# A decoder layer whose x also comes laid out with features on partitions, and whose vectors come as one table of columns

## The chip, the cores and the metric

One core of one Trainium2 chip runs the kernel. The metric is the device time of one execution in microseconds (us). The host lays weights out before the launch; that is not timed.

Engines: PE is TensorE (PEld its weight loads), DVE is VectorE, ACT is ScalarE, POOL is GpSimd, SP is SyncE, which here only issues DMAs. A queue of DMA issues is marked with a q (SPq, ACTq).

## What is computed

One layer on 256 tokens of 1024 features, in float32:

```
xn = rmsnorm(x, g1)
aq, ak, av, mq, mk, mv, mo, mi, mf, ga, gm = split(xn @ w_in)
ya = attention(aq, ak, av)                        # 8 heads of 64, causal
qk = silu(causal_conv(concat(mq, mk), conv_w, conv_b))
ym = rmsnorm(sigmoid(mo) * mlstm(qk, mv, mi + b_i, mf + b_f), gml)
h  = x + (sigmoid(ga + b) * (ya @ w_up_a) + sigmoid(gm + b) * (ym @ w_up_m)) @ w_out
h  = h + moe(rmsnorm(h, g2))                      # 32 experts, top group, top 2 in it
h  = h + (p @ w_proj) * sigmoid(rmsnorm(h, g3) @ w_gate)
out = rmsnorm(h, g_final)
```

## The kernel before, in words

All loads but one go out on SP's queue in program order. Big tiles live in a ring of ten slots of 2 MB (`slot`), so a late load waits until an earlier tile is done with. DMAs take semaphores in rotation: a new DMA on SP also waits until the one eight places before it has landed.

The front of the kernel is the mixing part. x is loaded in two halves into `h`, with tokens on partitions, between the pieces of the first weight, mq (L73 to L76). PE transposes it, 16 times 128x128, into PSUM (`transpose_x`, L252). For each of the eight k tiles (128 features each, L289) ScalarE scales the transposed x by the norm's gain g1 and rounds it to a high part (L298), VectorE makes the low part, what is left (L299); ScalarE and VectorE split the weights of the tile the same way into `whi` (L304) and `wlo` (L305); and PE multiplies high by high, high by low and low by high (L307 to L309), twelve products of 256 columns for one k tile, into four accumulators `pmq`. `on_act` and `on_dve` fix the order of these on ScalarE and VectorE.

The norm's 1/rms is not needed for that. Squares of `h` are summed on ScalarE (`square_x`, L277, four operations of 128x512), VectorE adds and scales the sums (L280, L189), POOL takes the power (L190), PE spreads the result over a tile (`prt`, L284), VectorE copies it to `rT` (L285), and whatever leaves PSUM later is multiplied by `rT` (L547, L542).

Then come the two gates of the mLSTM (`if_gates`, L384): POOL clears a part of the scratch tile that the squares were written to (L386) and lays the small gate weights out in it (L387, L388), they are split like any others, PE projects them (`pif`, L330 to L332), and a chain of small operations on four partitions on VectorE (L395 to L409), with an exponential and a logarithm on ScalarE (L400, L401), gives `am`, which PE transposes (`pam`, L415). The projections of mk, aq, ak and so on follow (`chunk_T`, `proj_T`), each with splits of 128x512 (L219, L220). A depthwise convolution of the columns of mq and mk runs between them (`conv`, L361 to L367: one ScalarE step and three VectorE steps, `acc`, for each of eight tiles). Where the program leaves the order open, the scheduler sets it.

Vectors (gains, biases, convolution weights) are loaded as 76 rows of 128 (L91), transposed by PE in one go and copied to the table `cols` (`load_columns`, L243); g1 has its own small load and transpose (L68, L234), the gate biases two loads (L101, L102). Before all this PE runs three products of 512 columns on an identity (L230), whose result nobody uses.

After the mixing part comes the expert part: 32 experts, 6 MB of weights each, loaded through the ring, then a last gate and norm.

Of the kernel before, what the change touches and what calls it, by code (L numbers as in the profile page):

```python
# [8 lines left out]
F32 = mybir.dt.float32  # L9
# [5 lines left out]
OP = mybir.AluOpType  # L15
# [19 lines left out]
NWARM0 = 3  # L35
# [12 lines left out]
def layer(ctx: ExitStack, tc: tile.TileContext, A, dbg=None):  # L48
    nc = tc.nc
    mm = nc.tensor.matmul  # L50

    const = ctx.enter_context(tc.tile_pool(name="const", bufs=1))
# [4 lines left out]
    fc = front.enter_context(tc.tile_pool(name="fc", bufs=1))  # L57

    def slot(shape, dt=F32, name="wt"):

        return ring.tile(shape, dt, name=name, tag="ring")


    h = keep.tile([P, NB, D], F32, name="h")
    y = keep.tile([P, NB, D], F32, name="scratch", tag="y")
    x_v = A["x"].rearrange("o (b p) d -> p (o b) d", p=P)
    g1r = fc.tile([KD, P], F32, name="g1r")
    nc.scalar.dma_start(out=g1r, in_=A["mix_norm_g"].rearrange("o (k p) -> (o k) p", p=P))  # L68
# [10 lines left out]
    rows = fc.tile([76, P], F32, name="rows")
    col_of = {}  # L80
    r0 = 0
    for nm, src in (
            ("g2", A["ffn_norm_g"].rearrange("o (k p) -> (o k) p", p=P)),
            ("g3", A["ple_norm_g"].rearrange("o (k p) -> (o k) p", p=P)),
            ("cb", A["conv_b"].rearrange("o (k p) -> (o k) p", p=P)),
            ("cw", A["conv_w"].rearrange("o c (k p) -> (o c k) p", p=P)),
            ("gml", A["mlstm_norm_g"].rearrange("o (k p) -> (o k) p", p=P)),
            ("bg", A["b_gate"].rearrange("o (k p) -> (o k) p", p=P)),
    ):
        n = src.shape[0]  # L90
        nc.sync.dma_start(out=rows[r0:r0 + n], in_=src)  # L91
        col_of[nm] = r0
        r0 += n
# [138 lines left out]

    pg1 = psf.tile([P, 512], F32, name="pg1", tag="tp")
    after(nc.tensor.transpose(pg1[:, 0:KD], g1r, ident[0:KD, 0:KD]), warm0)  # L234
    g1c = fc.tile([P, KD], F32, name="g1c")
    g1_copy = nc.vector.tensor_copy(out=g1c, in_=pg1[:, 0:KD])
    cols = const.tile([P, 76], F32, name="cols")
# [5 lines left out]
    def load_columns():  # L243
        pcol = psf.tile([P, 512], F32, name="pcol", tag="tp")
        nc.tensor.transpose(pcol[:, 0:76], rows, ident[0:76, 0:76])
        nc.vector.tensor_copy(out=cols, in_=pcol[:, 0:76])
        nc.vector.tensor_scalar(bgh, cols[:, col_of["bg"]:col_of["bg"] + 16], 0.5, None, op0=OP.mult)
# [4 lines left out]
    def transpose_x(k):  # L252
        pt = psf.tile([P, 2, T], F32, name="pt", tag="tp")
        for kk in range(2):
            for b in range(NB):
                after(nc.tensor.transpose(pt[:, kk, b * P:(b + 1) * P], h[:, b, (k + kk) * P:(k + kk + 1) * P], ident),
                      warm0)
        return pt
# [5 lines left out]
    seq = {"act": first_act, "dve": g1_copy}  # L264
# [5 lines left out]
    def on_dve(ins):  # L270
        after(ins, seq["dve"])
# [38 lines left out]
    load_columns()  # L310
# [726 lines left out]
    for b in range(NB):  # L1037
# [17 lines left out]
_INS = ["x", "p", "mix_norm_g", "w_mix", "w_if", "b_gate", "conv_w", "conv_b", "mlstm_if_b", "mlstm_norm_g",  # L1055
        "w_up", "w_out", "ffn_norm_g", "router_group_w", "router_group_b", "router_expert_w", "router_expert_b",
        "expert_gu", "expert_down", "ple_norm_g", "w_ple_gate", "w_ple_proj", "final_norm_g"]


def _laid_out(inputs):  # L1060
# [6 lines left out]

    w_in = a.pop("w_in")[0]
# [28 lines left out]
```

## Time and profile before

| | |
|---|---|
| median of 3 runs | 706.53 us (705.92 to 706.98) |
| the profiled execution | 706.04 us |
| its span, first to last instruction | 704.3 us |
| PE busy | 560.9 us (80%) |
| VectorE busy | 280.7 us (40%) |
| ScalarE busy | 186.1 us (26%) |
| DMA | 241.98 MB, 344 GB/s in the mean |
| chain that ended last | DMA 48%, PE 44% |

Everything but the first line is from one profiled execution, with times counted from the start of its span; its own time is 0.5 us below the median. Busy shares are means over stages with different limits, so they don't tell what a change in one stage is worth; for that the stage itself is read.

### The profile page before, as it was taken

What the parts mean: (1) busy time and instruction counts of PE and PEld (TensorE: products, weight loads), DVE (VectorE), ACT (ScalarE), POOL (GpSimd) and SP (SyncE); (2) the same over time, 40 slices, a digit from 0 to 9 for tenths busy, and PEclk for the clock granted to TensorE, in tenths of its full rate; (3) what the DMA queues carried; (4) which work ended last, traced back from release to release, by engine and by line L of the source; (5) the groups of instructions that cost most, each with busy time, mean ns of one, the idle gap of its engine ahead of it and who ended that gap; (6) DMA issues with size and microseconds to landing.
All of it is one profiled execution on the core that took longest, in us unless ns stands there. A gap on an engine that the chain in (4) does not pass through costs nothing.

```text
span 704.3 us, 12210 instructions
## 1 busy us (share of the span) xinstructions
PE 560.9 (80%) x5161; PEld 382.3 (54%) x5161; DVE 280.7 (40%) x684; ACT 186.1 (26%) x423; POOL 38.2 (5%) x59
## 2 busy tenths in 40 slices
PE   7999999999999998685686564967746956765894
PEld 7898778899986554342334231733423433432384
DVE  4898667676665343141022024312211310311175
ACT  6675556465453211001000000010000210000163
POOL 3000000001300000000000000000000000000063
PEclk9999999999999999899669886898978997988998
DMA  7946533338777899999999997999999999999921
GB/s 268 429 205 248 228 122 120 120 120 333 305 327 299 333 428 428 428 424 429 423 428 426 430 426 316 429 423 430 426 426 424 425 427 427 429 428 424 419 99 60
DMA packets 22130, 241.98 MB, mean 344 GB/s; under 512 B 4708, under 2 KB 5304, under 8 KB 7096
## 3 DMA queue, kind: packets, MB, share of 16 engines
q1 hardware_dynamic: 22056, 241.16, 82.5%
q8 instruction: 42, 0.69, 0.4%
q14 instruction: 16, 0.13, 0.0%
q10 hardware_dynamic: 16, 0.00, 0.0%
HBM read 240.10 MB, written 1.05 MB: 342 GB/s over the span
## 4 chain that ended last, share of the span: by engine, by line
DMA 48%; PE 44%; DVE 4%; ACT 2%; issue 1%; POOL 1%; POOLq 0%; SPq 0%; DVEq 0%; ACTq 0%
DMA wt<-in_expert_gu 31%; DMA wt<-in_expert_down 17%; PE pg L810 5%; PE po L330 4%; PE po L331 4%; PE po L332 4%; PE ps L839 3%; PE po L347 2%; PE po L346 2%; PE po L348 2%; PE pd L827 2%; PE px L761 2%; PE ps L923 1%; PE pyy L470 1%; DMA wt<-in_w_mix 1%
## 5 line engine op out<-in xcount | busy, mean ns | idle before, releaser
L810 PE MATMUL pg<-wt,xe 128*32 128x256 f32 x2032 | 153.6, 438 | 69.8 <-DMA wt<-in_expert_gu 69.8
L810 PEld LDWEIGHTS pg<-wt,xe 128*32 128x32 f32 x2032 | 73.3, 122 | 136.8 <-issue 55.6
L827 PE MATMUL pd<-wt,hT 128*32 128x256 f32 x1024 | 73.6, 434 | 22.8 <-DMA wt<-in_expert_down 18.6
L833 DVE COPY eo<-pd 32x256 f32<-32x256 f32 x64 | 27.1, 423 | 114.5 <-ACT eo L835 114.4
L827 PEld LDWEIGHTS pd<-wt,hT 128*32 128x32 f32 x1024 | 37.9, 121 | 47.4 <-issue 32.9
L835 ACT ACTIVATE eo<-pd 32x256 f32<-32x256 f32 x64 | 23.9, 374 | 150.3 <-PE pd L827 132.0
L816 DVE TENSOR_TENSOR hid<-sg,pg 128x128 f32<-128x128 f32 x32 | 9.2, 288 | 126.0 <-ACT sg L814 126.0
L220 DVE TENSOR_TENSOR wlo<-wt,whi 128x512 fp32r<-128x512 f32 x76 | 51.5, 685 | 18.3 <-ACT whi L219 18.1
L219 ACT ACTIVATE whi<-wt 128x512 fp32r<-128x512 f32 x77 | 47.3, 626 | 32.0 <-PE po L348 16.7
L814 ACT ACTIVATE sg<-pg 128x128 f32<-128x128 f32 x32 | 8.9, 277 | 168.7 <-PE pg L810 168.6
L761 PE MATMUL px<-og,y 128*128 128x128 f32 x256 | 39.6, 308 | 10.3 <-DVE og L752 6.8
L761 PEld LDWEIGHTS px<-og,y 128*128 128x128 f32 x256 | 35.5, 216 | 22.1 <-PEq L878 7.7
L839 PE MATMUL ps<-eo,dwT 128*128 128x512 f32 x64 | 34.2, 661 | 8.8 <-DVE eo L833 8.7
L332 PE MATMUL po<-XT,wlo 128*128 128x256 f32 x144 | 40.4, 280 | 1.0 <-DVE wlo L220 1.0
L330 PE MATMUL po<-XT,whi 128*128 128x256 f32 x144 | 40.6, 282 | 0.0
L331 PE MATMUL po<-XT,whi 128*128 128x256 f32 x144 | 40.3, 280 | 0.0
L765 DVE TENSOR_TENSOR xe<-px,cols 128x256 f32<-128x256 f32 x32 | 13.6, 424 | 61.5 <-PE pg L810 38.9
L220 POOL TENSOR_TENSOR glo<-wt,ghi 128x1024 fp32r<-128x1024 f32 x4 | 10.6, 2671 | 449.4 <-DMA wt<-in_w_ple_gate 448.6
L332 PEld LDWEIGHTS po<-XT,wlo 128*128 128x128 f32 x144 | 27.0, 188 | 1.2 <-DVE wlo L220 1.2
L220 DVE TENSOR_TENSOR spare<-wt,spare 128x512 fp32r<-128x512 f32 x34 | 23.3, 687 | 9.9 <-ACT spare L219 9.8
L331 PEld LDWEIGHTS po<-XT,whi 128*128 128x128 f32 x144 | 27.1, 188 | 0.2 <-issue 0.2
L330 PEld LDWEIGHTS po<-XT,whi 128*128 128x128 f32 x144 | 27.1, 188 | 0.0
(371 smaller groups left out, 956.9 us busy)
## 6 DMA issues: line engine op xcount, KB each, us to landing
wt<-in_expert_gu SPq DMA_DIRECT2D x63, 2048.0 KB, 38.2
wt<-in_expert_down SPq DMA_DIRECT2D x30, 2048.0 KB, 36.5
wt<-in_w_mix SPq DMA_DIRECT2D x10, 2048.0 KB, 22.2
wt<-in_w_up SPq DMA_DIRECT2D x2, 2048.0 KB, 8.5
wt<-in_w_out SPq DMA_DIRECT2D x2, 2048.0 KB
wt<-in_expert_down SPq DMA_DIRECT2D x4, 1024.0 KB
wt<-in_w_ple_gate SPq DMA_DIRECT2D x4, 1024.0 KB, 27.0
wt<-in_w_mix SPq DMA_DIRECT2D x4, 512.0 KB, 7.0
```

The costliest lines, as they stand in the source:

```text
L219: a = nc.scalar.activation(dst_hi, src, AF.Copy)
L220: b = (lo_on or nc.vector).tensor_tensor(dst_lo, src, dst_hi.bitcast(F32), op=OP.subtract)
L330: mm(out[:, f], whi[:, kk], ahi[:, k], start=(k == 0), stop=False)
L331: mm(out[:, f], whi[:, kk], alo[:, k], start=False, stop=False)
L332: mm(out[:, f], wlo[:, kk], ahi[:, k], start=False, stop=(k == kn - 1))
L346: mm(outs[b], ahi[:, k, bs], whi[:, k - k0], start=(k == 0), stop=False)
L761: ins = mm(px[:, k], y[:, b, kc:kc + P], og[:, b], start=(b == 0), stop=(b == NB - 1))
L810: ins = pe(mm(pg[32 * j:32 * j + 32], xe[:, k, 32 * i:32 * i + 32], gu[k][:, :, j * P:(j + 1) * P], start=(k == 0), stop=(k == KD - 1)))
L827: pe(mm(pd[32 * c:32 * c + 32], hT[:, 32 * j:32 * j + 32], dn[j][:, c * 256:(c + 1) * 256], start=(j == 0), stop=(j == 3)))
L833: nc.vector.tensor_copy(out=dst, in_=pd[32 * c:32 * c + 32])
L835: nc.scalar.activation(dst, pd[32 * c:32 * c + 32], AF.Copy)
L839: mm(ps, dwT[0:n, b], eo[0:n, c * 512:(c + 1) * 512], start=True, stop=True)
```

## The change

The host adds two inputs. `xT` is x with features on partitions, k tile by k tile; `cols` is a table of 85 columns with all vectors, g1 and the gate biases among them. xT is loaded into the first half of a ring tile, `QK`, which is not used for anything else until later, in five pieces that alternate with five pieces of mq. `h` follows as one load. The transposes of x and of the vectors, and the loads of the vectors, are gone; x is scaled and split straight from SBUF. PE runs five of its opening products instead of three. The square sums of `h` move from k tiles 2 and 5 to the place before k tile 6 and behind the loop, and with them the rest of the norm.

```diff
-NWARM0 = 3
+NWARM0 = 5
...
-    g1r = fc.tile([KD, P], F32, name="g1r")
-    nc.scalar.dma_start(out=g1r, in_=A["mix_norm_g"].rearrange("o (k p) -> (o k) p", p=P))
+    cols = const.tile([P, NC_], F32, name="cols")
+    nc.scalar.dma_start(out=cols, in_=A["cols"])
...
+    QK = slot([P, 2, 8, T], F32, name="QK")
+    aqk, qkc = QK[:, 0], QK[:, 1]
     wts = {"mq": slot([P, KD, 512])}
     mq_v = A["w_mix"][MIX.index("mq")]
-    for i in range(4):
-        if i < 2:
-            nc.sync.dma_start(out=h[:, :, i * 512:(i + 1) * 512], in_=x_v[:, :, i * 512:(i + 1) * 512])
-        nc.sync.dma_start(out=wts["mq"][:, 2 * i:2 * i + 2], in_=mq_v[:, 2 * i:2 * i + 2])
...
+    for k, n in ((0, 1), (1, 1), (2, 2), (4, 2), (6, 2)):
+        nc.sync.dma_start(out=aqk[:, k:k + n], in_=A["xT"][:, k:k + n])
+        nc.sync.dma_start(out=wts["mq"][:, k:k + n], in_=mq_v[:, k:k + n])
+    nc.sync.dma_start(out=h, in_=x_v)
...
-    pts = {}
     for k in range(KD):
-        if k in (0, 2, 3):
-            for kt in {0: (0, 2), 2: (4,), 3: (6,)}[k]:
-                pts[kt] = transpose_x(kt)
-        if k in (2, 5):
-            square_x(k // 4)
         if k == 6:
-            norm_x()
-        xt, g = pts[k // 2 * 2][:, k % 2], g1c[:, k:k + 1]
+            square_x(0)
+        xt, g = aqk[:, k], col("g1", k)
...
-    load_columns()
+    square_x(1)
+    norm_x()
+    nc.vector.tensor_scalar(bgh, cols[:, col_of["bg"]:col_of["bg"] + 16], 0.5, None, op0=OP.mult)
```

On SP's queue, at the start of the program (h is x with tokens on partitions, wt here is mq, then mk and the next five weights), before:

```order
L75 DMA h<-in_x 128x2x512
L76 DMA wt<-in_w_mix 128x1024
L75 DMA h<-in_x 128x2x512
L76 DMA wt<-in_w_mix 128x1024 x3
L91 DMA rows<-in_ffn_norm_g 8x128
L91 DMA rows<-in_ple_norm_g 8x128
L91 DMA rows<-in_conv_b 8x128
L91 DMA rows<-in_conv_w 32x128
L91 DMA rows<-in_mlstm_norm_g 4x128
L91 DMA rows<-in_b_gate 16x128
L99 DMA wif<-in_w_if 128x64
L101 DMA ifb<-in_mlstm_if_b 4x1
```

and in the change:

```order
L79 DMA QK<-in_xT 128x256
L80 DMA wt<-in_w_mix 128x512
L79 DMA QK<-in_xT 128x256
L80 DMA wt<-in_w_mix 128x512
L79 DMA QK<-in_xT 128x512
L80 DMA wt<-in_w_mix 128x1024
L79 DMA QK<-in_xT 128x512
L80 DMA wt<-in_w_mix 128x1024
L79 DMA QK<-in_xT 128x512
L80 DMA wt<-in_w_mix 128x1024
L81 DMA h<-in_x 128x2x1024
L85 DMA wif<-in_w_if 128x64
```

The load of h moved from the head of the queue to the place behind xT and mq, and eight small loads left it.

On ScalarE, from k tile 4 to the end of the k loop (XT is the scaled x, whi the weight split, scratch with ss a square with its sum), before:

```order
L298 ACTIVATE XT<-pt,g1c 128x256
L304 ACTIVATE whi<-wt 128x512
L277 ACTIVATE scratch,ss<-h 128x512 x2
L298 ACTIVATE XT<-pt,g1c 128x256
L304 ACTIVATE whi<-wt 128x512
L298 ACTIVATE XT<-pt,g1c 128x256
L304 ACTIVATE whi<-wt 128x512
L298 ACTIVATE XT<-pt,g1c 128x256
L304 ACTIVATE whi<-wt 128x512
L219 ACTIVATE whi<-scratch 128x512 x2
```

and in the change:

```order
L253 ACTIVATE XT<-QK,cols 128x256
L259 ACTIVATE whi<-wt 128x512
L253 ACTIVATE XT<-QK,cols 128x256
L259 ACTIVATE whi<-wt 128x512
L238 ACTIVATE scratch,ss<-h 128x512 x2
L253 ACTIVATE XT<-QK,cols 128x256
L259 ACTIVATE whi<-wt 128x512
L253 ACTIVATE XT<-QK,cols 128x256
L259 ACTIVATE whi<-wt 128x512
L238 ACTIVATE scratch,ss<-h 128x512 x2
L199 ACTIVATE whi<-scratch 128x512 x2
```

The last two squares, which stood ahead of tile 5, now stand behind tile 7, right ahead of the split of the gate weights; the first two stand ahead of tile 6.

On VectorE, from the copy of rT to the start of the gates' chain (RW takes the accumulators of mq, acc is a step of the convolution), before:

```order
L285 COPY rT<-prt 128x256
L220 TENSOR_TENSOR wlo<-scratch,whi 128x512
L547 TENSOR_TENSOR RW<-pmq,rT 128x256 x3
L246 COPY cols<-pcol 128x76
L547 TENSOR_TENSOR RW<-pmq,rT 128x256
L247 TENSOR_SCALAR bgh<-cols 128x16
L220 TENSOR_TENSOR wlo<-scratch,whi 128x512
L220 TENSOR_TENSOR wlo<-wt,whi 128x512
L363 SCALAR_TENSOR_TENSOR acc<-RW,cols,acc 128x256
L220 TENSOR_TENSOR wlo<-wt,whi 128x512
L395 TENSOR_TENSOR scratch<-pif,rT 4x256
```

and in the change:

```order
L200 TENSOR_TENSOR wlo<-scratch,whi 128x512 x2
L246 COPY rT<-prt 128x256
L200 TENSOR_TENSOR wlo<-wt,whi 128x512
L504 TENSOR_TENSOR RW<-pmq,rT 128x256 x4
L320 SCALAR_TENSOR_TENSOR acc<-RW,cols,acc 128x256 x3
L200 TENSOR_TENSOR wlo<-wt,whi 128x512
L320 SCALAR_TENSOR_TENSOR acc<-RW,cols,acc 128x256
L352 TENSOR_TENSOR scratch<-pif,rT 4x256
```

Four steps of the convolution, where one was, now stand ahead of the first operation of the gates' chain; the copy of the transposed vectors is gone, and the halving of the gate biases (bgh) has moved to the start of VectorE's list.

## Rows read from the trace of the kernel before

**Rows 1.** Stages: length; busy us of each engine; granted clock, DMA share, GB/s.

```profile
38.90:190.00 151.10, 150.80 (x1089) 133.49 (x1089) 108.72 (x244) 86.49 (x194) 9.29 (x15) 1.00 0.50 191
300.00:400.00 100.00, 68.19 (x717) 34.30 (x715) 21.60 (x56) 7.66 (x22) 0.00 (x0) 0.85 1.01 427
```

**Rows 2.** The chain that ended last: start us, length, what.

```profile
265.18 31.28 DMA wt<-in_expert_gu
```

**Rows 3.** Waits of PE, 0 to 60 us: waiter, releaser, us, times, longest.

```profile
PE pw L230 <- ACT identb L116: 3.1, 1, 3.1
PE pam L415 <- DVE scratch L409: 1.4, 1, 1.4
PE po L332 <- DVE wlo L220: 1.0, 1, 1.0
```

**Rows 4.** Timeline of PE: start us, length, engine, line, operation [idle before it].

```profile
4.70 1.97 PE L256 MATMUL pt<-ident,h 128*128 128x128 f32 x8
7.33 0.55 PE L307 MATMUL pmq<-XT,whi 128*128 128x256 f32 x1 [0.67 <-ACT whi L304]
...
12.16 0.28 PE L308 MATMUL pmq<-XT,whi 128*128 128x256 f32 x1
12.28 0.28 PE L309 MATMUL pmq<-XT,wlo 128*128 128x256 f32 x1
```

**Rows 5.** Timeline of SP's queue: loads that waited for an older load to land.

```profile
8.03 0.25 SPq L91 DMA_DIRECT2D rows<-in_mlstm_norm_g  x1
...
11.85 0.25 SPq L101 DMA_DIRECT2D ifb<-in_mlstm_if_b  x1
```

**Rows 6.** Stages as in rows 1, in the first loads.

```profile
2.00:7.00 5.00, 3.56 (x12) 2.02 (x12) 0.65 (x2) 1.95 (x4) 2.04 (x13) 1.00 0.89 312
8.00:9.00 1.00, 1.00 (x7) 1.00 (x7) 0.90 (x2) 1.00 (x4) 0.00 (x0) 1.00 1.06 434
```

**Rows 7.** Timeline of ScalarE: the last square and the pair after it.

```profile
14.54 0.62 ACT L277 ACTIVATE scratch<-h 128x512 f32<-128x512 f32 x1
...
15.15 0.46 ACT L298 ACTIVATE XT<-pt,g1c 128x256 fp32r<-128x256 f32 x1
...
15.51 0.62 ACT L304 ACTIVATE whi<-wt 128x512 fp32r<-128x512 f32 x1
...
16.03 0.47 ACT L298 ACTIVATE XT<-pt,g1c 128x256 fp32r<-128x256 f32 x1
```

**Rows 8.** Timeline, all engines: from the sums to the gate projection.

```profile
15.48 0.81 DVE L189 TENSOR_SCALAR r<-ss 128x2 f32<-128x2 f32 x1
...
16.38 1.07 POOL L190 TENSOR_TENSOR r<-r,mhalf 128x2 f32<-128x2 f32 x1
...
17.56 0.20 POOL L388 COPY scratch<-wif 128x32 f32<-128x32 f32 x1
...
21.97 0.37 PE L330 MATMUL pif<-XT,whi 128*128 128x256 f32 x1
```

**Rows 9.** That stretch of VectorE as in rows 1, and its timeline with PE's `pam`.

```profile
20.04:35.98 15.94, 13.70 (x114) 13.29 (x112) 14.12 (x32) 9.37 (x16) 0.30 (x1) 1.00 1.01 428
...
20.04 0.68 DVE L220 TENSOR_TENSOR wlo<-scratch,whi 128x512 fp32r<-128x512 f32 x1
...
23.37 0.69 DVE L220 TENSOR_TENSOR wlo<-wt,whi 128x512 fp32r<-128x512 f32 x1
23.97 0.48 DVE L363 SCALAR_TENSOR_TENSOR acc<-RW,cols,acc 128x256 f32<-128x256 f32 x1
24.37 0.69 DVE L220 TENSOR_TENSOR wlo<-wt,whi 128x512 fp32r<-128x512 f32 x1
...
25.08 0.41 DVE L395 TENSOR_TENSOR scratch<-pif,rT 4x256 f32<-4x256 f32 x1
...
35.70 0.28 DVE L409 COPY scratch<-scratch 4x256 f32<-4x256 f32 x1
...
36.13 0.28 PE L415 MATMUL pam<-ident,scratch 36*128 36x36 f32 x2 [1.39 <-DVE scratch L409]
```

More of the change, by code (lines that the diff above doesn't have):

```diff
@@ L66, in layer @@
     x_v = A["x"].rearrange("o (b p) d -> p (o b) d", p=P)
-    g1r = fc.tile([KD, P], F32, name="g1r")
-    nc.scalar.dma_start(out=g1r, in_=A["mix_norm_g"].rearrange("o (k p) -> (o k) p", p=P))
+    NC_ = 85
+    cols = const.tile([P, NC_], F32, name="cols")
+    nc.scalar.dma_start(out=cols, in_=A["cols"])
+    col_of = dict(g1=0, g2=8, g3=16, cb=24, cw=32, gml=64, bg=68)
+    ifb = cols[0:36, 84:85]
+    QK = slot([P, 2, 8, T], F32, name="QK")
+    aqk, qkc = QK[:, 0], QK[:, 1]
     wts = {"mq": slot([P, KD, 512])}
     mq_v = A["w_mix"][MIX.index("mq")]
-    for i in range(4):
-        if i < 2:
-            nc.sync.dma_start(out=h[:, :, i * 512:(i + 1) * 512], in_=x_v[:, :, i * 512:(i + 1) * 512])
-        nc.sync.dma_start(out=wts["mq"][:, 2 * i:2 * i + 2], in_=mq_v[:, 2 * i:2 * i + 2])
[L79 to L93, printed above, removed]
+    for k, n in ((0, 1), (1, 1), (2, 2), (4, 2), (6, 2)):
+        nc.sync.dma_start(out=aqk[:, k:k + n], in_=A["xT"][:, k:k + n])
+        nc.sync.dma_start(out=wts["mq"][:, k:k + n], in_=mq_v[:, k:k + n])
+    nc.sync.dma_start(out=h, in_=x_v)
     wif = fc.tile([P, KD, 8], F32, name="wif")
-    ifb = fc.tile([36, 1], F32, name="ifb")
     def load_if():
         nc.sync.dma_start(out=wif, in_=A["w_if"])
-        ifb_v = A["mlstm_if_b"].rearrange("o n -> n o")
-        nc.sync.dma_start(out=ifb[0:4], in_=ifb_v[0:4])
-        nc.sync.dma_start(out=ifb[32:36], in_=ifb_v[4:8])
     def load_cols(v):
@@ L126, in layer @@
     nc.gpsimd.memset(raw[:, :, 0:3], 0.0)
-    QK = slot([P, 2, 8, T], F32, name="QK")
-    nc.gpsimd.memset(QK[:, 0, 0, 0:1], 0.0)
-    aqk, qkc = QK[:, 0], QK[:, 1]
     VV = slot([P, 4096], F32, name="VV")
@@ L230, in layer @@
         warm0 = mm(pw, identb, identb[:, None, :].to_broadcast([P, 4, P]), start=True, stop=True)
[L233 to L237, printed above, removed]
     bgh = fc.tile([P, 16], F32, name="bgh")
@@ L241, in col @@
         return cols[:, col_of[nm] + i:col_of[nm] + i + 1]
[L243 to L247, printed above, removed]
-    pmq = [psf.tile([P, T], F32, name="pmq", tag="po" if f < 3 else "at", bufs=3) for f in range(4)]
[L252 to L258, printed above, removed]
+    pmq = [psf.tile([P, T], F32, name="pmq", tag="po" if f < 3 else "at", bufs=3) for f in range(4)]
     ss = small.tile([P, 2, NB], F32, name="ss", bufs=1)
@@ L262, in layer @@
     rT = fc.tile([P, T], F32, name="rT")
-    seq = {"act": first_act, "dve": g1_copy}
+    seq = {"act": first_act, "dve": None}
     def on_act(ins):
@@ L270, in on_dve @@
     def on_dve(ins):
-        after(ins, seq["dve"])
+        if seq["dve"] is not None:
+            after(ins, seq["dve"])
         seq["dve"] = ins
@@ L1052, in layer @@
     moe.close()
-_INS = ["x", "p", "mix_norm_g", "w_mix", "w_if", "b_gate", "conv_w", "conv_b", "mlstm_if_b", "mlstm_norm_g",
-        "w_up", "w_out", "ffn_norm_g", "router_group_w", "router_group_b", "router_expert_w", "router_expert_b",
-        "expert_gu", "expert_down", "ple_norm_g", "w_ple_gate", "w_ple_proj", "final_norm_g"]
+_INS = ["x", "xT", "p", "cols", "w_mix", "w_if", "w_up", "w_out", "router_group_w", "router_group_b",
+        "router_expert_w", "router_expert_b", "expert_gu", "expert_down", "w_ple_gate", "w_ple_proj", "final_norm_g"]
 def _laid_out(inputs):
@@ L1066, in cols @@
         return w.reshape(-1, P, w.shape[1] // n, n).transpose(2, 1, 0, 3)
+    a["xT"] = a["x"][0].T.reshape(KD, P, T).transpose(1, 0, 2)
+    vecs = [a.pop(nm).reshape(-1, P) for nm in ("mix_norm_g", "ffn_norm_g", "ple_norm_g", "conv_b", "conv_w",
+                                                "mlstm_norm_g", "b_gate")]
+    a["cols"] = _np.zeros((P, 85), _np.float32)
+    a["cols"][:, 0:84] = _np.concatenate(vecs).T
+    ifb = a.pop("mlstm_if_b").reshape(2, HM)
+    a["cols"][0:HM, 84], a["cols"][32:32 + HM, 84] = ifb[0], ifb[1]
     w_in = a.pop("w_in")[0]
```

## The prediction

> **What bounds the kernel now.** I read the stages first, then the chain that ended last, then PE's waits, then the first 40 us engine by engine. The stages [rows 1] show two regimes. From 38.9 to 190 us PE is busy 150.80 of 151.10 us; from 300 to 400 us the DMA engines are full (share 1.01, 427 GB/s). Where they meet, the chain [rows 2] goes over to a load of expert weights that starts at 265.18, when products of an earlier expert have freed its slot. So what delays or advances PE before 190 us moves the slots, with them the expert loads, and the end by as much: I carry a shift of the front to the end one to one. PE starts work at 3.1 us, when the identity is ready; after that it has two long waits [rows 3], 1.4 us before the small transposes `pam` of the input and forget gates and 1.0 on a weight split, and 0.67 before the first projection [rows 4]. All lie in the first 37 us, as does the whole change, so that stretch is the sum.
>
> **What the change removes.** PE: 16 transposes of x, one of g1, one of the 76 vector rows. Eight of the 16 run at 4.70, before the first weight has landed, and take 1.97 us at the slow pace [rows 4]; they cost nothing. The other eight, at twice that pace, are about 0.9 us of PE. SP loses six row loads and two gate biases, VectorE two copies. ScalarE and VectorE make the same splits as before, from SBUF rather than PSUM; I keep their durations. No wait in rows 3 is for one of the loads taken away, so they give nothing.
>
> **The start.** Before, the first product ran at 7.33, after 512 KB of x, there for the transposes at 4.70, and 512 KB of weights [rows 4]. In the change it needs the column table, 128 KB of xT and 256 KB of weights: 0.44 MB, where 0.52 MB had landed by 4.70. So these are there at about 4.6, and a split of 0.62 us follows [rows 7]. The warm products have 512 columns; with 256 columns products are 0.21 us apart at the slow pace (23 recorded from 7.33 to 12.16), so five warm ones take 2.1 us from 3.1. The first product is at 5.3, a lead of 2.0 us over 7.33. Were nothing else late, that and the 0.9 us of transposes would be the gain.
>
> **What is late next.** The square sums need x with tokens on partitions. That tile, h, was loaded first; now it is one transfer of 1.05 MB behind xT and mq. Small loads on SP waited before until an older load had landed, which dates these: x's second half is there by 8.03, the last piece of mq by 11.85 [rows 5], when 3.15 MB had come. In the change h is the end of 4.24 MB (xT 1.05, mq 2.10, h 1.05, the table 0.04). The extra 1.09 MB take 2.5 us at 434 GB/s [rows 6]; with a tenth or two for short rows **h lands at 14.5**, 6.5 us later than x did. The loads behind h are not late: SP gets to mk at about 7 us rather than 12.5, since the small loads are gone.
>
> On ScalarE two squares stand ahead of the scaling of k tile 6, and two more follow tile 7. ScalarE takes its list in order, so tiles 6 and 7 wait for h. Start to start, a square is 0.61 us and a pair of scaling and weight split 0.88 [rows 7]. From h: squares at 14.5 and 15.1, pair 6 at 15.7 with its split done at 16.75, pair 7 at 16.6, squares at 17.5 and 18.1. PE has 72 products for tiles 0 to 5. At worst it keeps the slow pace until 12.1, as in rows 4: 32 by then, 40 more at 0.12 by 16.8. So it reaches tile 6 no later than the weights do, at whatever time the clock rises, and the two added warm products decide nothing. The low half of tile 6, another split, is for PE 0.5 us behind; 24 products take 2.8; PE is through at 20.1.
>
> Then the chain of the norm. Before, the last square started at 14.54 and the gate weights were laid out by 17.76 [rows 7, 8]: 3.2 us, of which 0.81 is a tiny VectorE operation while POOL clears the scratch tile, and 1.07 the power. PE came to the gate projection (`pif`) only at 21.97, so 4.2 us of it were cover. In the change the same 3.2 us from 18.1 end at 21.3, one split of 0.62 follows, and PE starts `pif` at **22.2**. The cover is used up: the lead of 2.0 us has become a lag of 0.2, and PE stood still for some 2 us around the two transposes of the norm. The low half of the gate weights holds PE for 0.5 us, so `pif` ends at 25.5, where before it was read at 25.08 [rows 9].
>
> **VectorE.** What ended PE's longest wait before was VectorE: from the low half of the gate weights at 20.04 to the last copy of the gates at 35.70, with `pam` at 36.13 [rows 9]. In the 15.94 us to that copy's end it was busy 14.12. In the change the stretch starts at 22.2 (+2.2), has three convolution steps more ahead of that copy, 0.40 us each start to start (+1.2), and lacks two copies (-0.3). Of the idle 1.8 us I let 0.3 be filled, since most of it is a wait for ScalarE's exponential and logarithm, which stays: `pam` at 36.1 + 2.8 = 38.9. PE has done three products more by then, -0.35. That gives +2.5. Following split after split in the new order by the durations of rows 7 to 9 gives +2.7 at the end of mk, and on the way three weight splits that PE waits for by 0.6 to 1.2 us; I take **+2.7**. From there the lists of the two kernels are the same and VectorE is three steps ahead, so no new wait follows.
>
> **Sum.** The profiled execution took 706.04 us with a span of 704.3; the change makes this 708.7 and 707.0. The median of the runs shown is 706.53, 0.5 above, so **709.2**. The unknown is when h lands. If all bytes from 2 to 7 us had run at 434 instead of 312 GB/s [rows 6], they would take 1.4 us less: 13.1. If xT's 1.05 MB, in rows of 1 to 2 KB, ran at 312 throughout, 0.9 us more: 15.5. I stay at 14.5, to which the landings of rows 5 are nearest. The delay follows h one to one down to about 12, where PE, busy with the tiles until 18, is itself the last; so the forecast's own range, for h from 13.9 to 15.5, is 708.6 to 710.2.
>
> **The rivals.**
>
> *x comes sooner.* h lands at 13.1 as just worked out; tile 6 hardly waits, `pif` starts at 20.8, the net is +1.3: 707.8. For it: from 8 us on the loads do run at 434. Against it: the first loads of the change are in shorter rows than those that ran at 312. The Trainium skill, DMA: Bandwidth & Descriptors, Specifications, gives 435 GB/s as the ceiling of the fabric; were it reached from the start, this rival's time would come out. The trace agrees with the ceiling from 8 us on, and stays well below it before 7.
>
> *VectorE keeps up (not slower).* Before, the gate chain on VectorE started (25.08) as soon as `pif` was done. If it starts with `pif`'s end at 25.5 again, `pam` comes 0.4 us later, less the 0.35: 706.6. The point that decides is whether VectorE is through by then with what now stands ahead of the chain: four splits at 0.60, the copy of rT and four evacuations at about 0.4, four convolution steps at 0.40. I count 6.0 us from 22.2, so 28.2; it would have to be 2.7 less. With h at 12.5 as well, `pif` ends at 23.5, the chain starts 1.6 us sooner than before, and less the 0.35 the time is 704.6.
>
> *The clock falls.* PE waits about 1 us at tile 6 and 2 us around the norm. If it falls to the lower level (1.2 GHz) there, products go at 0.21 instead of 0.12 for as long as from 7.33 to 12.16: 22 products, 2.1 us, part of it behind VectorE's delays: 711. Against it: through the 1.0 and 1.4 us of rows 3 the granted clock reads 1.00 [rows 9]. The Trainium skill, TensorE: Matmul & The Clock Gate, HAM oscillation, has waits between bursts of products bring the clock down to half; the trace shows no such fall after waits this short.
>
> **How the numbers follow.** Forecast 0.60; x sooner 0.17; VectorE keeps up 0.10; both together 0.06; the clock 0.07. A measurement of this kernel can tell about 0.2%, 1.4 us, from no change. The forecast and the clock count as slower (0.67), x sooner and VectorE alone as the same (0.27), both together as faster (0.06). The range leaves out the last and the clock's case: 706.2 to 710.8.
>
> **What would show it.** Right: ScalarE's longest early wait is for h, before the first square, and ends between 14 and 15.5; the first product is near 5.3; PE waits before tile 6 and before the transposes of the norm; `pif` starts near 22.2, `pam` near 38.9; and PE has no wait from 42 us on. Wrong: h there by 12, or VectorE's gate chain starting with `pif`'s end.

## The result, and the profile after

| | before | changed |
|---|---|---|
| median | 706.75 us (705.92 to 707.03) | 714.55 us (713.35 to 715.05) |
| ratio, 95% interval | | 1.0111 [1.0099, 1.0123] |
| the profiled execution | 706.04 us | 714.41 us |
| its span | 704.3 us | 712.4 us |
| PE busy | 560.9 us | 564.7 us |

The change costs 7.8 us. The forecast was 709.2 with a range up to 710.8: the sign was right, the size was not. Line numbers below are those of the kernel that a row is from; in the changed one the middle of the program stands 43 lines higher.

TensorE's waits, 0 to 60 us, in the changed kernel (as in [rows 3]: us, times, longest):

```profile
PE pmq L262 <- ACT whi L259: 3.3, 2, 2.2
PE pif L287 <- DVE RW L504: 3.2, 1, 3.2
PE pw L210 <- ACT identb L99: 2.9, 1, 2.9
PE pam L372 <- DVE scratch L366: 1.6, 1, 1.6
PE pmq L264 <- DVE wlo L260: 0.4, 2, 0.2
PE prt L245 <- POOL r L170: 0.4, 1, 0.4
```

Against [rows 3] two long waits are new: 2.2 us before a product of a k tile and 3.2 us before `pif`, and the second ends with VectorE's `RW`, the evacuation of `pmq`. (Of the 3.3 us in the first line, the other 1.1 stand before tile 2, at 10.82: the loads of the first tiles were late too.) In time order on TensorE:

```profile
5.32 0.55 PE L262 MATMUL pmq<-XT,whi 128*128 128x256 f32 x1
...
19.47 0.39 PE L262 MATMUL pmq<-XT,whi 128*128 128x256 f32 x1 [2.20 <-ACT whi L259]
...
27.14 0.36 PE L287 MATMUL pif<-XT,whi 128*128 128x256 f32 x1 [3.23 <-DVE RW L504]
...
28.41 0.33 PE L288 MATMUL pif<-XT,whi 128*128 128x256 f32 x1
28.53 0.42 PE L289 MATMUL pif<-XT,wlo 128*128 128x256 f32 x1
28.74 0.42 PE L287 MATMUL pif<-XT,whi 128*128 128x256 f32 x1
...
42.33 0.28 PE L372 MATMUL pam<-ident,scratch 36*128 36x36 f32 x2 [1.62 <-DVE scratch L366]
```

The first product came at 5.32 (forecast 5.3), the first of tile 6 at 19.47, `pif` at 27.14 (forecast 22.2), `pam` at 42.33 (38.9). The rows around 28.5 show the distance of two products going from 0.12 to 0.21 us. The stages (columns as in [rows 1]) say why, in the third number from the right, the granted clock:

```profile
2.00:7.00 5.00, 4.00 (x12) 2.13 (x13) 1.80 (x5) 3.02 (x6) 2.01 (x13) 1.00 0.90 265
7.00:10.00 3.00, 2.74 (x19) 2.53 (x18) 1.18 (x2) 0.51 (x1) 0.00 (x0) 1.00 0.96 293
...
28.00:30.00 2.00, 2.00 (x13) 2.00 (x13) 1.68 (x4) 0.75 (x2) 0.00 (x0) 0.63 0.98 418
30.00:32.00 2.00, 2.00 (x12) 2.00 (x11) 1.00 (x4) 0.61 (x1) 0.00 (x0) 0.52 0.98 418
32.00:34.00 2.00, 2.00 (x19) 2.00 (x19) 1.91 (x5) 0.66 (x2) 0.00 (x0) 1.00 1.04 442
```

Between 28 and 32 us TensorE was at the lower level, 1.2 GHz, for most of the time. The first two lines show the other trouble: 265 and 293 GB/s, where the kernel before had 312 [rows 6] and 420:

```profile
7.00:10.00 3.00, 2.67 (x12) 2.70 (x13) 2.00 (x4) 3.00 (x9) 0.00 (x0) 1.00 1.03 420
```

So h came late in the changed kernel. ScalarE's list:

```profile
13.68 0.62 ACT L259 ACTIVATE whi<-wt 128x512 fp32r<-128x512 f32 x1
17.17 0.63 ACT L238 ACTIVATE scratch<-h 128x512 f32<-128x512 f32 x1 [2.87 <-DMA h<-in_x]
...
18.80 0.61 ACT L259 ACTIVATE whi<-wt 128x512 fp32r<-128x512 f32 x1
...
20.86 0.61 ACT L238 ACTIVATE scratch<-h 128x512 f32<-128x512 f32 x1
```

The first square of h started at 17.17, after a wait of 2.87 us for that load; tiles 6 and 7 (whose weights are split at 18.80 and after) stood behind it. And VectorE, from the gate weights on:

```profile
24.43 1.29 DVE L200 TENSOR_TENSOR wlo<-scratch,whi 128x512 fp32r<-128x512 f32 x2 [0.81 <-ACT whi L199]
25.64 0.42 DVE L246 COPY rT<-prt 128x256 f32<-128x256 f32 x1
25.98 0.68 DVE L200 TENSOR_TENSOR wlo<-wt,whi 128x512 fp32r<-128x512 f32 x1
26.58 1.41 DVE L504 TENSOR_TENSOR RW<-pmq,rT 128x256 f32<-128x256 f32 x4
...
31.55 0.41 DVE L352 TENSOR_TENSOR scratch<-pif,rT 4x256 f32<-4x256 f32 x1 [0.96 <-PE pif L289]
```

`rT`, which could have been copied at 24 (its transposes started at 23.48), stands behind two splits that wait for ScalarE; the evacuation `RW` stands behind `rT` and one more split. Only when the first of its four parts was done could `pif` start, at 27.14.

The router's first load, the same program point in both kernels, tells what of this the front handed on. Before:

```profile
158.54 0.38 SPq L208 DMA_DIRECT2D wr<-in_router_group_w  x1
```

Changed:

```profile
165.40 0.38 SPq L188 DMA_DIRECT2D wr<-in_router_group_w  x1
```

6.9 of the 8.1 us by which the spans differ are there at 165 us; PE had no long wait between 43 and that point.

### The profile page after: what moved, and what is told of

It reads as the page before. It is cut to its first block, busy times and chain, and to the rows that moved or that the text cites. A ratio compares the mean times of both kernels' runs of the same rounds, so it can differ in the third digit from the quotient of the medians.

```text
span 712.4 us, 12173 instructions
## 1 busy us (share of the span) xinstructions
PE 564.7 (79%) x5145; PEld 382.5 (54%) x5145; DVE 281.9 (40%) x682; ACT 187.6 (26%) x423; POOL 37.0 (5%) x58
## 5 line engine op out<-in xcount | busy, mean ns | idle before, releaser
L784 PE MATMUL pd<-wt,hT 128*32 128x256 f32 x1024 | 76.6, 449 | 21.4 <-DMA wt<-in_expert_down 16.5
L718 PE MATMUL px<-og,y 128*128 128x128 f32 x256 | 38.0, 300 | 7.7 <-DVE og L709 4.0
## 6 DMA issues: line engine op xcount, KB each, us to landing
wt<-in_w_mix SPq DMA_DIRECT2D x10, 2048.0 KB, 15.5
```

The costliest lines, as they stand in the source:

```text
L718: ins = mm(px[:, k], y[:, b, kc:kc + P], og[:, b], start=(b == 0), stop=(b == NB - 1))
L784: pe(mm(pd[32 * c:32 * c + 32], hT[:, 32 * j:32 * j + 32], dn[j][:, c * 256:(c + 1) * 256], start=(j == 0), stop=(j == 3)))
```

## The experiments

All ratios are to the kernel before, on the same chip; the changed kernel's is 1.0111. Gains in us are differences of medians from 714.55; by the ratios they come out between 0.9 us smaller (d_sq) and 0.5 larger (c_bank).

### What waits for h

**d_sq**: the first pair of squares goes behind the tiles.

```diff
-        if k == 6:
-            square_x(0)
...
+    square_x(0)
     square_x(1)
     norm_x()
```

> The changed kernel with the first pair of squares behind tile 7 instead of ahead of tile 6 on ScalarE's list, so that no tile waits for h. Theory (h lands at 17.1 and holds tiles 6 and 7, and with them the norm): the wait of 2.2 us before tile 6 goes, TensorE is through with the tiles by 20.5, the four squares run from 17.2 to 19.8, r is there 1.6 to 2 us sooner, and the time falls by 1.6 to 3 us: 711.5 to 713. Rival, the gate product's wait for VectorE's list eats it (its order is the scheduler's, and may change): within 0.7 us of 714.5.

Measured: 710.45 us (709.07 to 713.37), ratio 1.0065 [1.0045, 1.0084]: 4.1 us back, more than expected. TensorE:

```profile
20.98 0.43 PE L245 MATMUL prt<-ident,r 128*128 128x128 f32 x2 [0.97 <-POOL r L170]
...
23.11 0.36 PE L286 MATMUL pif<-XT,whi 128*128 128x256 f32 x1 [1.69 <-DVE RW L503]
```

No wait before tile 6, `pif` at 23.11 after a wait of 1.69, and the granted clock stays at 1.00 from 2 to 110 us. The scheduler also set VectorE's list anew (`rT` now ahead of the gate weights' splits, one convolution step ahead of the gates' chain where the changed kernel has four), so that this run undoes a part of the next cause too.

**n_noh**: the squares read other data, already there, so the sums are not those of x; no engine's list changes.

```diff
-            on_act(nc.scalar.activation(y[:, b, cs], h[:, b, cs], AF.Square, accum_out=ss[:, i, b:b + 1]))
+            on_act(nc.scalar.activation(y[:, b, cs], aqk[:, 2 * b:2 * b + 2], AF.Square, accum_out=ss[:, i, b:b + 1]))
```

> The changed kernel with the squares read from the transposed x's first four pieces instead of h, in the same places of ScalarE's list and of the same size; h is loaded as before. The sums of squares are thus of other numbers, and the output is not the reference's. Theory (h at 17.1 is the root of all that comes late in the front): no wait before tile 6, r ready by 18 to 19, TensorE through with the tiles at 20 to 20.7, pif starts at 21 to 22 with no wait of over 0.7 us and the clock does not fall; what is left over the kernel before is the tiles' other place: 707 to 709. Rival, VectorE's list or the slower loads of the first tiles cost by themselves: pif at 23 or later, 711 or more.

Measured: 711.93 us, 1.0074 [1.0061, 1.0087]: the rival's side (711 or more, `pif` at 23 or later). The theory wanted 707 to 709 and failed in this form. `pif`:

```profile
23.99 0.55 PE L287 MATMUL pif<-XT,whi 128*128 128x256 f32 x1 [3.23 <-DVE RW L504]
```

It starts 3.15 us sooner, as it should, but the wait before `pif` is the same 3.23 us as with h late. It is therefore a cost of its own, not h's. And the clock fell twice, though no tile waited for h:

```profile
24.00:26.00 2.00, 2.00 (x9) 2.00 (x10) 2.00 (x6) 0.98 (x2) 0.00 (x0) 0.50 1.02 434
...
42.00:44.00 2.00, 2.00 (x12) 2.00 (x11) 1.67 (x3) 1.82 (x5) 0.00 (x0) 0.50 0.97 402
```

**o_pieces**: the first loads in 3 pairs instead of 5.

```diff
-    for k, n in ((0, 1), (1, 1), (2, 2), (4, 2), (6, 2)):
+    for k, n in ((0, 2), (2, 2), (4, 4)):
```

> The changed kernel with the loads of the transposed x and of mq in 3 pairs (2, 2 and 4 k tiles each) instead of 5 (1, 1, 2, 2, 2): rows of 2 to 4 KB and 4 to 8 KB per partition instead of 1 to 2 KB and 2 to 4 KB. Theory (the short rows hold the loads at 232 to 265 GB/s between 2 and 7 us, where the kernel before had 307 to 312): over 290 GB/s there, h lands by 15.5 to 16.3 instead of 17.1, the first product comes 0.7 to 1.5 us later, and the time is 712.5 to 714. Rival, the rate is that of two streams side by side whatever their rows: under 270 GB/s, h at 17.0 or later, 714.5 to 716.

Measured: 711.41 us, 1.0074 [1.0061, 1.0087], better than either theory said. The first product came 1.3 us later, at 6.60, yet h was there at 14.75, where the prediction had it:

```profile
14.75 0.63 ACT L238 ACTIVATE scratch<-h 128x512 f32<-128x512 f32 x1 [0.95 <-DMA h<-in_x]
```

```profile
2.00:7.00 5.00, 2.71 (x7) 1.01 (x7) 1.23 (x4) 2.51 (x6) 2.00 (x13) 1.00 0.93 282
7.00:10.00 3.00, 3.00 (x15) 2.84 (x15) 2.57 (x6) 2.24 (x5) 0.00 (x0) 1.00 1.02 410
...
28.00:30.00 2.00, 2.00 (x12) 2.00 (x11) 1.09 (x2) 0.15 (x1) 0.00 (x0) 0.50 1.10 467
```

The rate between 7 and 10 us went from 293 to 410 GB/s. So the small pieces held the loads up (this run changes their number and the length of their rows together), and following them tile by tile cost more than it gave. `pif` still waited 3.23 us, and in this run the clock was down from 24 to 30 us, so that the 2.4 us gained at h did not all arrive.

**f_hfirst**: h goes out behind the second piece; the squares stand ahead of tiles 3 and 5 and the norm ahead of tile 6 (2, 5 and 6 in the kernel before).

```diff
-    nc.sync.dma_start(out=h, in_=x_v)
+        if k == 1:
+            nc.sync.dma_start(out=h, in_=x_v)
...
+        if k in (3, 5):
+            square_x(k // 4)
         if k == 6:
-            square_x(0)
+            norm_x()
...
-    square_x(1)
-    norm_x()
```

> The changed kernel with h issued behind the second piece instead of last, and the squares and the norm back at the tiles where the kernel before has them (ahead of tiles 3, 5 and 6). Theory (the late h is the root: norm, evacuation and gate product follow it): h lands at 8 to 9.5, the tiles behind it 2.4 to 3.5 us later, the last at about the 17.1 at which h landed; r is there before TensorE is through with the tiles at 19.5 to 21, and pif starts at 20.5 to 22 as in the kernel before: 706.5 to 709, with the 1.5 to 2 us of the tiles' place still in it. Rival, the tiles' longer wait for the loads costs as much as h did, and TensorE's clock falls in it: 711 to 714.

Measured: 710.62 us, 1.0053 [1.0038, 1.0067]: between the theory's 709 and the rival's 711, nearer the rival. The squares no longer waited for h, but tile 2 was late:

```profile
11.77 0.51 ACT L256 ACTIVATE XT<-QK,cols 128x256 fp32r<-128x256 f32 x1 [3.49 <-DMA QK<-in_xT]
```

TensorE waited 3.21 us before it, and the clock was low from 13 to 19 us. Moved ahead, h holds up the tiles instead of the norm.

**g_xnorm**: the sums of squares from the transposed x, by POOL and TensorE; h loaded behind the projection's weights.

```diff
...
+    def square_k(k):
+        nc.gpsimd.tensor_tensor(xsq[:, k], aqk[:, k], aqk[:, k], op=OP.mult)
...
+    def sum_k():
+        for b in range(NB):
+            for k in range(KD):
+                mm(pss[:, 2 * b:2 * b + 1], xsq[:, k, b * P:(b + 1) * P], ones_e[:, 0:1],
+                   start=(k == 0), stop=(k == KD - 1))
...
```

> The changed kernel with the sum of squares taken from the transposed x: POOL squares each 128x256 piece, TensorE sums them over the partitions by 16 products with a column of ones, and h, which then only the residual needs, is loaded behind the projection's weights. Theory (h is the root, and its 1 MB is in the way of nothing else): no wait for h is left, the 16 short products cost 1 to 2 us of TensorE ahead of tile 7, TensorE is through by 21, r is there at about the same time, pif starts at 21 to 23: 706 to 709, with the place of the tiles in it. Rival, the norm's own chain (VectorE, POOL, TensorE, VectorE: 3.2 us) behind the last squares is late and pif still waits over 2 us for the evacuation: 710 to 712.

Measured: 716.66 us, 1.0141 [1.0119, 1.0163], slower than everything. The scheduler put the sums' products at the head of TensorE's list, where they waited for POOL's squares:

```profile
PE pss L243 <- POOL VV L238: 8.5, 3, 4.7
```

The first product of a tile came at 11.89. It tells nothing on h.

### The wait before the gate product

**c_bank**: `pif` in a free PSUM buffer.

```diff
-        pif = psf.tile([P, 2, T], F32, name="pif", tag="po", bufs=3)
+        pif = psf.tile([P, 2, T], F32, name="pif", tag="tp")
```

> The changed kernel with pif in one of the two PSUM buffers that the transposes of x have left free, so that it no longer needs the first evacuation of pmq. Theory: pif starts when its weights are split, at 24.4 to 24.6 instead of 27.1, ends at 27.5, TensorE's clock does not fall, and if that wait is the price, the time is 710.5 to 711.5. Rival, VectorE is the bound there (it still has the same work ahead of the gate chain, and idled only 0.96 us for pif and 0.3 before): the wait goes over to pam, and the time is 713.2 to 713.8. Rival, nothing hangs on it: 714.5.

Measured: 712.66 us (710.69 to 713.28), 1.0077 [1.0064, 1.0090], between the theory's 710.5 to 711.5 and the rival's 713.2 to 713.8:

```profile
24.25 0.39 PE L287 MATMUL pif<-XT,whi 128*128 128x256 f32 x1 [0.54 <-ACT whi L199]
```

The wait is gone and `pif` starts 2.9 us sooner, with h as late as in the changed kernel (17.0). That shows the cause of the wait: the buffer of the first `pmq`, freed by VectorE. But `pam` waited 1.6 us, as it does in the changed kernel, and the clock fell there instead:

```profile
40.00:42.00 2.00, 2.00 (x12) 2.00 (x11) 0.14 (x2) 1.97 (x4) 1.32 (x2) 0.50 1.00 426
```

So of 2.9 us (3.4 at `pam`) 1.9 arrive. The 3.4 are not the buffer's alone: the scheduler set VectorE's list anew, and none of the four convolution steps stands ahead of the gates' chain in this run.

### The clock

**b_fill**: 14 products without dependences in that wait.

```diff
...
+        for _ in range(14):
+            fill = mm(pfill, identb, identb[:, None, :].to_broadcast([P, 4, P]), start=True, stop=True)
+            after(fill, last)
+            last = fill
```

> The changed kernel with 14 dependence-free products of 512 columns (0.213 us each at the full clock, 3.0 us) on TensorE between the transposes of r and the gate product pif, in the time in which TensorE waits 3.2 us; they take nothing from anyone and pif's start stays at 27.1. Theory of the clock: pif's 24 products stay at 0.12 us apart instead of falling to 0.21 at 28.5, pif ends 1.4 us sooner, and the gate chain on VectorE, which waited 0.96 us for it, starts 1 to 1.4 us sooner: 713.0 to 713.6. Rival, VectorE has other work ready that fills its wait, so nothing is gained: 714.5. Rival, the wait itself is the only cost: 714.5 too, with pif still slow.

Measured: 713.16 us (713.04 to 714.03), 1.0098 [1.0084, 1.0113]. The intervals of this and the changed kernel overlap, and in the profiled execution h was there 0.6 us sooner (16.57), so what the fill is worth in the end can't be told; the pace is plain. First and last product of `pif`:

```profile
26.55 0.36 PE L292 MATMUL pif<-XT,whi 128*128 128x256 f32 x1 [0.21 <-DVE RW L509]
...
29.35 0.28 PE L294 MATMUL pif<-XT,wlo 128*128 128x256 f32 x1
```

24 products in 2.9 us with the clock at 1.00 throughout, against 4.2 us before the next tile's first product in the changed kernel. The Trainium skill, TensorE: Matmul & The Clock Gate, HAM oscillation, describes this cost of waits between bursts; these traces agree, at half clock and 1.3 us for these 24 products.

### The place of the tiles

Taking rows out of one pool and columns into another moved every later tile. The ring's ten slots, into which the experts' weights are loaded, are 16384 bytes apart; the last of them stood at 183488 bytes per partition before and stands at 183520 in the changed kernel.

**a_pad**: 32 bytes more per partition in the constants' pool of the changed kernel.

```diff
+    pad = const.tile([P, 8], F32, name="pad")
+    nc.gpsimd.memset(pad, 0.0)
```

> The changed kernel with 32 bytes more per partition in the pool of constants, which moves every later tile by 32 bytes and puts the weight tiles whi and wlo, XT and the ring back on addresses that are multiples of 64, as in the kernel before; nothing else changes. Theory of place: the products with whi and wlo as weights between 43 and 60 us go from 0.119 us apart back to 0.114, which over all the projections is 1.5 to 2 us: 712.5 to 713.0. Rival, the place of the destination also slows the loads (265 GB/s between 2 and 7 us where the kernel before had 312): the tiles come sooner as well, h lands before 16, and the time is under 711.5. Rival, the place means nothing: 714.5, and the distances stay.

Measured: 710.17 us (709.69 to 710.82), 1.0054 [1.0041, 1.0067]: 4.4 us back, but not where I looked for it. The front is unchanged (`pif` at 27.33, the router's load at 165.56), and the products with whi are as far apart as in the changed kernel (0.119 us), so the theory of place named the wrong thing. The experts' loads are faster (last number, GB/s; 426 and 421 in the changed kernel):

```profile
300.00:340.00 40.00, 28.26 (x321) 14.82 (x313) 10.27 (x28) 2.72 (x8) 0.00 (x0) 0.93 1.01 431
440.00:500.00 60.00, 42.00 (x492) 26.27 (x495) 17.72 (x55) 4.49 (x13) 0.00 (x0) 0.91 1.01 429
```

**e_bpad**: the same 32 bytes in the kernel before; they put its ring where the changed kernel has it.

```diff
     cols = const.tile([P, 76], F32, name="cols")
+    pad = const.tile([P, 8], F32, name="pad")
+    nc.gpsimd.memset(pad, 0.0)
```

> The kernel BEFORE with 32 bytes more per partition in the pool of constants, which takes whi, wlo, XT and the ring off the multiples of 64 and puts the tile spare onto them, as the change did; nothing else. Theory of place: the products with whi and wlo as weights go from 0.114 to 0.119 us apart, 1.5 to 2 us in all: 708.2 to 708.8. If the loads are slowed too (under 300 GB/s between 2 and 7 us), over 709.5. Rival, the place means nothing: 706.7.

Measured: 707.22 us, 1.0007 [0.9998, 1.0016], no difference that can be told: the rival's side. So the ring's place is not what made the changed kernel 7.8 us slower.

**m_b64**: 64 bytes, `const.tile([P, 16], ...)`, in the place of the 32.

> The kernel BEFORE with 64 bytes more per partition in the pool of constants: every later tile moves by 64 bytes, the ring from 183488 to 183552, which is a multiple of 128; nothing else. The two kernels whose ring stood there so far (the changed one with 32 bytes more, and the one with only the table) moved the experts' weights at 428 to 431 GB/s, the others at 425 to 426. Theory of place for the loads: 429 to 431 GB/s between 300 and 600 us here too, 2.5 to 3.5 us less: 703.3 to 704.3, and then the table of columns alone is worth nothing (its kernel ran at 704.3). Rival, the address has no part in it and the table's kernel gained by the missing small loads: 706.7.

Measured: 703.51 us (702.78 to 703.68), 0.9956 [0.9943, 0.9969], the side of the theory. The kernel before with one unused tile:

```profile
300.00:340.00 40.00, 27.33 (x296) 14.11 (x294) 10.41 (x28) 3.19 (x9) 0.00 (x0) 0.91 1.01 430
440.00:500.00 60.00, 46.02 (x560) 27.63 (x563) 17.43 (x52) 5.15 (x15) 0.00 (x0) 0.93 1.01 430
```

**q_192**: 192 bytes, `const.tile([P, 48], ...)`.

> The kernel BEFORE with 192 bytes more per partition in the pool of constants: the ring stands at 183680, a multiple of 128 but not of 256 (64 bytes more, which gave 703.5, had made it a multiple of both). If multiples of 128 are what the loads like: 429 GB/s between 300 and 600 us and 703 to 704.3. If it takes 256: 425 to 426 GB/s and 706.3 to 707.3.

Measured: 706.10 us, 1.0000 [0.9991, 1.0009], so it takes 256:

```profile
300.00:340.00 40.00, 27.29 (x309) 14.57 (x301) 11.11 (x30) 3.46 (x10) 0.00 (x0) 0.94 1.01 428
440.00:500.00 60.00, 46.97 (x519) 25.85 (x517) 16.35 (x50) 5.14 (x15) 0.00 (x0) 0.85 1.01 428
```

| last slot at | modulo 256 | GB/s, 300 to 340, 440 to 500 us | 300 to 600 us | kernels |
|---|---|---|---|---|
| 183488 | 192 | 426, 427 | 420 | before |
| 183520 | 224 | 426, 421 | 419 | changed |
| 183520 | 224 | 424, 427 | 419 | e_bpad |
| 183680 | 128 | 428, 428 | 420 | q_192 |
| 183552 | 0 | 430, 430 | 423 | m_b64 |
| 183552 | 0 | 431, 429 | 423 | a_pad |

The short windows differ by up to 5 GB/s within one kernel; the long one is steadier: of all sixteen kernels of this document, the five with the ring on a multiple of 256 (h_cols, l_both and p_three are the others) have 423 GB/s from 300 to 600 us, the eleven others 418 to 420. The bytes moved every other tile too, so that it is the ring's place is the nearest reading, not a separate test. The Trainium skill, DMA: Bandwidth & Descriptors, How a descriptor splits into AXI transactions, says that a descriptor is cut at 256-byte boundaries and that one that starts past a boundary fetches, unused, the bytes between the boundary and its start; it does not speak of tiles in SBUF. Carried over to a row of 16 KB that lies 192 bytes past a boundary, that makes, as an estimate from the page, 1.2% more; the traces have 0.7% (423 to 420).

**h_cols**: only the table of columns, in the kernel before, with the ring at 183552.

```diff
-    g1r = fc.tile([KD, P], F32, name="g1r")
-    nc.scalar.dma_start(out=g1r, in_=A["mix_norm_g"].rearrange("o (k p) -> (o k) p", p=P))
+    cols = const.tile([P, 85], F32, name="cols")
+    nc.scalar.dma_start(out=cols, in_=A["cols"])
...
-        xt, g = pts[k // 2 * 2][:, k % 2], g1c[:, k:k + 1]
+        xt, g = pts[k // 2 * 2][:, k % 2], col("g1", k)
...
```

> The kernel BEFORE with only the table of columns (the rows' and vectors' small loads, their two transposes and copies gone; 32 bytes added so that the tiles stand on multiples of 64); x goes its old way. Theory (the loss is all in x's way): 705.5 to 706.7, the small loads having been beside the others. Rival, the table's load of 340-byte rows on ScalarE's queue, ahead of the first tile, delays x: 707.5 or more.

Measured: 704.30 us, 0.9967 [0.9956, 0.9977]. That is no better than m_b64, which has the place without the table: the table alone is worth nothing that can be told, and what its run gained was the place.

### All together

**l_both**: squares behind the tiles, h in two halves, the gate weights laid out in a tile of their own, the gate product ahead of the norm in a free buffer, 32 bytes.

```diff
...
-    nc.sync.dma_start(out=h, in_=x_v)
+    for i in range(2):
+        nc.sync.dma_start(out=h[:, :, i * 512:(i + 1) * 512], in_=x_v[:, :, i * 512:(i + 1) * 512])
...
+    pif = if_proj()
+    square_x(0)
+    square_x(1)
+    norm_x()
...
```

> The changed kernel mended in what the runs point to, all at once: 32 bytes more in the pool of constants, h in two halves, the squares behind tile 7, the gate product's weights prepared in a tile of their own and its products ahead of the norm's transposes, in one of the two free PSUM buffers, so that nothing of it waits for the norm. Theory: no wait before tile 6, TensorE through with the tiles by 19.5 to 20.5, pif right behind it and at the full clock until 22.3 to 23.3, the first product of mk after the evacuation at 23.2 to 24.5 (24.7 in the kernel before), the loads of the experts at 429 GB/s: 701 to 703.5, under both kernels. Rival, mk's load (behind h) or VectorE's list holds the products of mk: 704 to 706.

Measured: 707.24 us (704.68 to 708.54), 1.0007 [0.9996, 1.0019]; the theory failed. It left the loads in five small pieces:

```profile
11.74 0.38 PE L263 MATMUL pmq<-XT,whi 128*128 128x256 f32 x1 [1.71 <-ACT whi L260]
...
27.16 0.36 PE L286 MATMUL po<-XT,whi 128*128 128x256 f32 x1 [1.54 <-DVE RW L510]
```

Tile 2 came late again, the clock was low from 12.7 to 16, the tiles were done at 22.4 instead of 20, and `RW`, now later than `pif`, held mk's first product until 27.16.

**p_three**: o_pieces and c_bank, the gate weights laid out in a tile that the squares don't write, and the 32 bytes.

```diff
...
+    for k, n in ((0, 2), (2, 2), (4, 4)):
...
-        wif32 = y[:, 1].rearrange("p (k n) -> p k n", k=KD)
+        wif32 = VV[:, 0:1024].rearrange("p (k n) -> p k n", k=KD)
...
+        pif = psf.tile([P, 2, T], F32, name="pif", tag="tp")
```

> The changed kernel with three mends of one line each and the 32 bytes: the loads in 3 pairs (2, 2 and 4 k tiles) as in o_pieces, pif in a free PSUM buffer as in c_bank, and the gate product's weights laid out in a tile that the squares don't write, so that POOL need not wait for them. Squares and norm stay where the change has them. Theory (the loss is the sum of h's late landing through the loads in short rows, pif's wait for VectorE's first evacuation, and the clock that falls in these waits): h lands by 15, no wait on TensorE of over 1 us between the first product and pif, pif starts at 20.8 to 21.5, no stretch at half clock after 12 us, the router's loads are issued at 157.5 to 159 (158.5 in the kernel before), and with the experts' loads at 429 GB/s the time is 702 to 704. Rival, something of the change remains that none of the three holds: the router's loads at 160 or later, 705 or more.

Measured: 703.27 us (702.94 to 703.47), 0.9955 [0.9942, 0.9969], as expected. TensorE's waits until 60 us:

```profile
PE pw L212 <- ACT identb L101: 2.9, 1, 2.9
PE pmq L264 <- ACT whi L261: 1.4, 1, 1.4
PE pam L374 <- DVE scratch L368: 1.4, 1, 1.4
PE po L291 <- DVE wlo L202: 0.9, 1, 0.9
```

Between the first product (6.61) and `pam` there is only the 0.9 on a weight split, which the kernel before has too. VectorE's scaling of the sums, and `pif`:

```profile
19.30 0.17 DVE L171 TENSOR_SCALAR r<-ss 128x2 f32<-128x2 f32 x1
...
20.55 0.36 PE L289 MATMUL pif<-XT,whi 128*128 128x256 f32 x1
```

The granted clock reads 1.00 from 2 to 110 us, and the router's load goes out at 158.59, where it was 158.54 before. So the loss of the front is whole in what these mends take away. They take away more than the late h, the wait for the buffer and the falls of the clock, though. The gate weights are split at 18.98, ahead of the norm, so `pif` hangs on h no longer; this third mend was not run by itself. And the scheduler puts all four convolution steps behind the start of the gates' chain, as in c_bank. With the ring at the same place, the mended change (703.27) and the kernel before (703.51, m_b64) are equal: laid out by the host or transposed on the chip, x costs this kernel the same. Both are faster than the kernel before and the changed one.

## Why the prediction was wrong, and where it was right

**Right.** The start: 5.32 for 5.3. The mechanism: h last, two squares ahead of tile 6, the lead lost and more. VectorE's gate chain: 10.7 us from its start to `pam` in the forecast (28.2 to 38.9), 10.8 measured (31.55 to 42.33). After 42 us PE had no wait to speak of, and the front's shift went on to the end.

**First wrong step: "with a tenth or two for short rows h lands at 14.5".** It landed at 17.1. I added h's bytes at 434 GB/s to a time read from a kernel whose rows are longer; five pairs of small pieces ran at 265, then 293. With three pairs the same bytes were there at 14.75 (o_pieces). The upper bound, 15.5, took xT alone at 312; the slower rate held for all that shared the queue with it, and was lower. The rival "x comes sooner" leaned on 434 from the start; the changed kernel's trace is farthest from that just there.

**Second: "one split of 0.62 follows, and PE starts `pif` at 22.2".** That counted the gate weights and forgot the result's place. `pif` takes the PSUM buffer of the first `pmq`, free only after VectorE's evacuation, which needs `rT`. Before, this was covered: the evacuation had begun at 21.08, and `pif` started at 21.97 without a wait for it [rows 8]. In the change r was ready at 23.4 and `pif` started 3.7 us later. n_noh shows this wait without h's delay, c_bank h's delay without this wait.

**Third: "the clock falls", given 0.07.** It fell. "Through the 1.0 and 1.4 us of rows 3 the granted clock reads 1.00" was true of two waits with long work before them, and no evidence for waits of 2.2 and 3.2 us close together. Its price, 1.7 us by the granted clock of the two stages, was near the 2.1 worked out, but I had it as a rival to the late h, and the two came together. It doesn't need h: in n_noh the clock fell too.

**In sum**, `pam` was 6.2 us late instead of 2.8. VectorE's chain began at 31.55 for 28.2: most of that is h's 2.7 passed on, and 0.96 is its wait for `pif`, which the buffer and the clock had made late. Until the router came 1.0 more that no step had: `pam` to the router's load took 123.07 us for 122.41, and PE had three products fewer left (0.35). There, part is a distance: from 43 to 64 us (37 to 58 before) products with whi or wlo as weights were 0.119 us apart (0.113 to 0.114), in `spare`, another tile, 0.117 (0.117). The kernel before with nothing but padding has 0.117 to 0.118 and takes as long from `pam` to the router as the changed one (e_bpad 123.07, q_192 123.08, m_b64 123.11), so 0.7 of the 1.0 comes of where the tiles stand, not of x; which rule sets it stays open. The last 1.2 us, after the router's load (547.0 for 545.8), lie within what the kernels with the ring off a multiple of 256 differ by there: 545.4 to 547.0.

The mends' single gains (3.1, 1.9, 4.1, and 2.6 for n_noh) don't add up: the clock fell in n_noh, o_pieces and c_bank, where another wait was left, though not in d_sq, and VectorE's list was another in c_bank and d_sq. How much of the 7.8 us belongs to each is therefore not settled; that the mends of p_three together undo all of the front's loss is shown.

## What to carry to other kernels

When a step moves, ask of each product not only when its operands are there but whose PSUM buffer it takes and what frees it; order lists show the wait, and its cover can vanish. A pipeline cut into pieces that follow their loads pays only if the pieces don't slow the loads. Before crediting a change with a gain or a loss, see where it has pushed the tiles: 32 bytes were worth more here than the whole layout of x.

## What the runs showed of the hardware that was not expected

- Loads of the experts' 16 KB rows ran at 423 GB/s from 300 to 600 us with the ring on multiples of 256 bytes and at 418 to 420 elsewhere; over this kernel that is 0.44% (m_b64).
- VectorE's operation on 128x2 numbers that scales the sums took 0.81 us while POOL cleared the scratch tile [rows 8], and 0.17 in p_three and l_both, where POOL was not at work beside it.
- With one wait mended, the fall of the clock came at another: 28 us in the changed kernel, 40 us in c_bank, 24 and 41 us in n_noh.
- In the opening the products were 0.21 us apart while the column of the granted clock read 1.00 (the pace is in [rows 4], the column in [rows 6]); in the later falls, at the same distance, the column showed 0.50. So it is no proof of full pace in the first 12 us.
